# The first three MLP blocks of a decoder trunk: another order of TensorE's products

## The chip, the core and the metric

The kernel runs on one core of a Trainium2 chip. A core has five engines that run side by side and wait for each other through semaphores: TensorE (PE in the profile) multiplies matrices, VectorE (DVE) and ScalarE (ACT) work on single elements, GpSimd (POOL) and SyncE (SP) here mainly issue DMA transfers. TensorE reads from SBUF and writes to PSUM, which has 8 banks; a matmul can add to what stands in a bank. The metric is the time of one execution in microseconds of the device.

## The reference

Two decoder layers over 512 tokens of width 1024, in float32. The change lies in the MLP, which each layer ends with:

```python
def sq_relu_mlp(xn, w_up, w_down):
    hid = jnp.square(jax.nn.relu(xn @ w_up))
    return hid @ w_down

for i in range(DEPTH):                      # DEPTH = 2
    ...                                     # a mixer: attention in layer 0, gated linear attention in layer 1
    x = x + sq_relu_mlp(rms_norm(x, norm_mlp[i]), mlp_w_up[i], mlp_w_down[i])
```

`w_up` is 1024 x 4096 and `w_down` 4096 x 1024.

## The kernel before

**Numbers.** TensorE's fast format holds fewer bits than float32, so each operand is cut into a high and a low part: ScalarE rounds to the high part (`wh`, line 112), VectorE subtracts it and keeps the low part (`wl`, line 115). A product of two such operands is three matmuls: high with high, high with low, low with high. The function `piece` cuts one piece of weights; there are three buffers each for `wh` and `wl`.

**Blocks.** `up_block(b)` computes 512 of the 4096 hidden features for all tokens, for b = 0 to 7. It treats the product as a 2 x 2 block product and does it with seven products instead of eight, in the manner of Strassen and Winograd. The weights of a block are four quarters a11, a12, a21, a22 of 512 rows by 256 columns (512 KB each), and sums of them; the inputs are quarters of the normed x and sums of those, ready before the MLP starts (`x0h` to `x7l`, and `T0h` to `T3l` for the sums T1 to T4). One product, `product(bank, weights, name, begin)`, is 24 matmuls of 128 x 128 weights by 256 columns: 16 with `wh`, then 8 with `wl`. The steps of a block, each with its product:

- s1: product 11 of a11, into a bank x1 (three such banks, tag "u"). Its result also seeds the running sum: `seed` has ScalarE copy it into the bank b2. There is one such bank (tag "seed").
- s2: product 21 of a12, added to x1. `finish` then scales it and clips it on VectorE (line 889) and squares it on ScalarE (line 890), into the hidden tile q.
- s5: product T1 of s = a21 + a22, into a bank x5; ScalarE copies it away as p5. In blocks 2 to 7 this step also loads a12, computes s (line 931) and has GpSimd's queue load a11 on top of a21.
- s6: VectorE makes s := s + a11 (line 948). Product T2 of s is added to the running sum b2; ScalarE copies the sum away as u2.
- s3: VectorE makes a12 := a12 + s (line 954). Product 22 of a12 is added to x5; VectorE adds u2 to it (line 957), and `finish`.
- s7: product T3 of a21 (a11 was added to it on loading) is added to the running sum b2; VectorE reads b2 and adds p5 (line 963), and `finish`.
- s4: product T4 of a22 is added to the running sum b2, and `finish`.

An engine that reads a bank and TensorE that writes it wait for each other.

**Order.** The order in which the steps are called sets the order of instructions on each engine. Blocks 0 and 1 begin interleaved (s1, s1, s2, s2); block 1's first sum is kept as p1 in SBUF, since the bank b2 belongs to block 0 then, and `seed` copies it in at its s6. From there each block ran to its end: s5, s6, s3, s7, s4. From block 2 on, steps of `down_block` (the second matrix, products of hidden tiles `h` with 48 matmuls each) stand between the steps. Weights of block 2 and later come through five buffers (tag "raw", 512 KB each); SP's queue issues the loads in order, each when a buffer is free.

Of the kernel before, what the change touches and what calls it, by code (L numbers as in the profile page):

```python
# [15 lines left out]
ALU = mybir.AluOpType  # L16
# [33 lines left out]
def trunk_kernel(ctx: ExitStack, tc: tile.TileContext, t_in: dict, out: bass.AP, out_row: bass.AP):  # L50
    nc = tc.nc
    PE, ACT, DVE, POOL, SP = nc.tensor, nc.scalar, nc.vector, nc.gpsimd, nc.sync
# [15 lines left out]
    def pool_of(name):  # L68
        return now[name][1]
# [3 lines left out]
    def uname(s):  # L73
        count[0] += 1
        return f"{s}_{count[0]}"
# [34 lines left out]
    def split(src, hi, lo, hi_eng=ACT, lo_eng=DVE, order=lambda i: i):  # L110
        if hi_eng is ACT:
            raised.append(order(ACT.activation(hi, src, AF.Copy)))  # L112
        else:
            hi_eng.tensor_copy(hi, src)
        return lo_eng.tensor_tensor(lo, src, f(hi), ALU.subtract)  # L115
# [29 lines left out]
    def piece(raw, a, n, order=lambda i: i):  # L145
        hi = sb.tile([P, a, n], F32R, tag="wh", bufs=3, name=uname("wh"))
        lo = sb.tile([P, a, n], F32R, tag="wl", bufs=3, name=uname("wl"))
        cut_at.append(split(raw, hi, lo, order=order))
        return hi, lo
# [658 lines left out]
    def mlp(layer, nrm, nxt, final=False):  # L808
        w_up, w_dn = t_in["mlp_w_up"][layer], t_in["mlp_w_down"][layer]
        quad = nrm.quad  # L810
        NB = FF // FB
# [11 lines left out]
        def matmuls(p, w, k0, ks, ms, x, begin, end):  # L823
            def one(i, j, k, m, start, stop):
                return PE.matmul(  # L825
                    p[:, m * TH : (m + 1) * TH],
                    w[i][:, k - k0, m * P : (m + 1) * P],
                    x[k][j],
                    start=start,
                    stop=stop,  # L830
                    skip_group_check=True,
                )

            steps = [(k, m) for k in ks for m in ms]
            for k, m in steps:
                i = one(0, 0, k, m, begin and k == 0 and m % 2 == 0, False)
                if (k, m) == steps[0]:
                    tc.keep_in_program_order(i)
                one(0, 1, k, m, False, False)
            for k, m in steps:  # L840
                one(1, 0, k, m, False, end and k == 3)
# [3 lines left out]
        def up_block(b):  # L845
            fh, s = b % 2, b // 2
            q = []

            def outputs():
                q.extend(pool_of("down").tile([P, 4, TH], F32, tag="q", bufs=6, name=uname("q")) for _ in range(2))  # L850
                Q[s, fh] = q

            def unit(half, trail):
                if half and b < 2:
                    return wide[b][trail]
                return fill(up.tile([P, KH, 256], F32, tag="raw", bufs=5, name=uname("raw")), half, trail)

            def rows(half, trail):
                c0 = b * FB + half * 256
                return w_up[trail * 512 : trail * 512 + 512, c0 : c0 + 256].rearrange("(k p) n -> p k n", p=P)  # L860

            def fill(t, half, trail):
                with tc.issue_after(wide["last"].ins) if "last" in wide and b > 1 else nullcontext():
                    i = SP.dma_start(t, rows(half, trail))
                if half and b < 2:
                    wide["last"] = i
                return t

            def fill_sums(s):
                v["s"] = s  # L870
                fill(s, 1, 0)
                joint(s, 1, 1)
                fill(wide[b][0], 1, 0)
                joint(wide[b][0], 0, 0)
                fill(wide[b][1], 1, 1)

            def joint(t, half, trail):
                POOL.dma_start(t, rows(half, trail), accum_op=ALU.add)  # L878

            fills.append(fill_sums)  # L880

            def product(p, a, name, begin):
                w = v.pop(name) if name in v else piece(a, KH, 256)
                matmuls(p, w, 0, range(KH), range(2), quad[name], begin, True)

            def finish(c, half, tk):
                qs = q[tk is second][:, 2 * half : 2 * half + 2]
                r = nrm.rstd[:, tk].unsqueeze(1).to_broadcast([P, 2, TH])
                DVE.scalar_tensor_tensor(qs, c, 0.0, r, ALU.min if half else ALU.max, ALU.mult)  # L889
                ACT.activation(qs, qs, AF.Square)  # L890

            def pairs(t):
                return t.rearrange("p (j t) -> p j t", j=2)

            def mt():
                return pool_of("down").tile([P, 512], F32, tag="mt", bufs=4, name=uname("mt"))

            v = made[b] = {}

            def s0():  # L900
                v["a11"], v["a12"] = unit(0, 0), unit(0, 1)
                if b == 0:
                    for name, a in (("11", v["a11"]), ("21", v["a12"])):
                        v[name] = piece(a, KH, 256)
                else:
                    w = v["11"] = tuple(up.tile([P, KH, 256], F32R, tag=f"T{KH - 1}{x}", name=uname("w")) for x in "hl")
                    split(v["a11"], *w)

            def s1():
                outputs()  # L910
                if "a11" not in v:
                    v["a11"] = unit(0, 0)
                a = v["a11"]
                v["a21"], v["a22"] = unit(1, 0), unit(1, 1)
                v["x1"] = bank("u")
                product(v["x1"], a, "11", True)
                if b == 1:
                    v["p1"] = mt()
                    ACT.activation(v["p1"], v["x1"], AF.Copy)
                else:  # L920
                    seed(v["x1"])

            def seed(src):
                v["b2"] = pool_of("mps").tile([P, 512], F32, tag="seed", name=uname("ps"))
                ACT.activation(v["b2"], src, AF.Copy)

            def s5():
                if "s" not in v:
                    v["s"] = up.tile([P, KH, 256], F32, tag="raw", bufs=5, name=uname("raw"))
                    v["a12"] = unit(0, 1)  # L930
                    DVE.tensor_tensor(v["s"], v["a21"], v["a22"], ALU.add)  # L931
                    joint(v["a21"], 0, 0)
                s = v["s"]
                v["x5"] = bank("u")
                product(v["x5"], s, "T1", True)
                v["p5"] = mt()
                ACT.activation(v["p5"], v["x5"], AF.Copy)

            def s2():
                if "a12" not in v:  # L940
                    v["a12"] = unit(0, 1)
                product(v["x1"], v["a12"], "21", False)
                finish(pairs(v["x1"]), 0, first)

            def s6():
                if b == 1:
                    seed(v["p1"])
                DVE.tensor_tensor(v["s"], v["s"], v["a11"], ALU.add)  # L948
                product(v["b2"], v["s"], "T2", False)
                v["u2"] = mt()  # L950
                ACT.activation(v["u2"], v["b2"], AF.Copy)

            def s3():
                DVE.tensor_tensor(v["a12"], v["a12"], v["s"], ALU.add)
                product(v["x5"], v["a12"], "22", False)
                c = q[1][:, 0:2]
                DVE.tensor_tensor(c, pairs(v["x5"]), pairs(v["u2"]), ALU.add)
                finish(c, 0, second)

            def s7():  # L960
                product(v["b2"], v["a21"], "T3", False)
                c = q[1][:, 2:4]
                DVE.tensor_tensor(c, pairs(v["b2"]), pairs(v["p5"]), ALU.add)  # L963
                finish(c, 1, second)

            def s4():
                product(v["b2"], v["a22"], "T4", False)
                finish(pairs(v["b2"]), 1, first)

            return [s0, s1, s2, s5, s6, s3, s7, s4] if b < 2 else [s1, s5, s2, s6, s3, s7, s4]  # L970

        def down_block(s):
            last = s == NB // 2 - 2
# [155 lines left out]

        made = {}  # L1130
        blocks = [up_block(b) for b in range(NB)]
        for b in range(2):
            blocks[b].pop(0)()
# [29 lines left out]
        for b in range(2):  # L1163
            blocks[b].pop(0)()
        downs = []
        for b in range(NB):
            for i, step in enumerate(blocks[b]):
                step()
                if downs and (i % 2 or (b % 2 and i == 6)):
                    downs.pop(0)()  # L1170
            if b % 2 and b < NB - 1:
                downs += down_block(b // 2)
# [579 lines left out]
```

## Time and profile before

| | |
|---|---|
| three runs | 1067.56, 1068.91 and 1069.22 us, median 1068.91 |
| profiled execution | 1068.29 us; its span, from the first to the last instruction, 1066.6 us |
| TensorE busy | 1048.6 us, 7322 matmuls |
| VectorE busy | 856.7 us |
| ScalarE busy | 640.1 us |
| products at line 825, up and down, of both layers | about 192 to 465 us and 739 to 1012 us of the span |
| TensorE's granted clock, mean | 0.996 of full speed |

A row of the timeline gives the start in us, the duration, the engine, the line, the operation, the tiles written and read, the count, and in brackets the idle time before it with what ended it. Matmuls overlap in their pipeline: a row's duration of 0.28 us is not its cost, which is the distance from start to start.

### The profile page before, as it was taken

The numbers are of one execution on the slowest core, as the hardware profiler recorded it, in microseconds if no ns is written. First come the engines' busy times: TensorE is split into PE (matmuls) and PEld (weight loads), VectorE is DVE, ScalarE is ACT, GpSimd is POOL, SyncE is SP. The second block draws the span as 40 slices with busy tenths as digits, with TensorE's granted clock in tenths as the row PEclk, the third lists the DMA queues.
The fourth block names the chain that finished last, engine by engine and source line by source line (L and its number), as shares of the span: only waits on it lengthen the run. The fifth ranks groups of instructions, "written<-read, shape, count | busy, mean of one in ns | idle before, by whom it ended". The sixth has DMA issues, their size and how long they took to land.

```text
span 1066.6 us, 17924 instructions
## 1 busy us (share of the span) xinstructions
PE 1048.6 (98%) x7322; PEld 967.8 (91%) x7322; DVE 856.7 (80%) x1185; ACT 640.1 (60%) x934; POOL 77.9 (7%) x104
## 2 busy tenths in 40 slices
PE   8999999999999999999999999999999999999997
PEld 6788888989999999998788888888999999999986
DVE  6789879899899789966565654668999799799865
ACT  6577645665666776654334734655666667775734
POOL 6400000000000000030000000001000000000000
PEclk9999999999999999999999999999999999999999
DMA  6412016865554663351122212238564555653412
GB/s 204 105 50 79 1 40 196 180 179 137 166 139 132 178 147 117 94 193 43 50 80 80 80 48 71 80 98 216 163 137 139 169 129 158 187 128 103 139 39 80
DMA packets 113874, 126.76 MB, mean 119 GB/s; under 512 B 8592, under 2 KB 85664, under 8 KB 113792
## 3 DMA queue, kind: packets, MB, share of 16 engines
q1 hardware_dynamic: 98048, 107.62, 31.7%
q0 software_dynamic: 13792, 16.80, 10.1%
q10 hardware_dynamic: 1952, 1.21, 0.4%
q8 instruction: 57, 0.93, 0.4%
q14 instruction: 25, 0.20, 0.1%
HBM read 123.51 MB, written 2.10 MB: 118 GB/s over the span
## 4 chain that ended last, share of the span: by engine, by line
PE 93%; DVE 5%; DMA 1%; issue 1%; ACT 0%; SPq 0%; DVEq 0%
PE ps L825 46%; PE ps L120 13%; PE ps L122 13%; PE ps L121 13%; PE ps L137 2%; DVE wl L115 2%; PE ps L1406 2%; DMA wraw_ckv<-in_mla_w_in_dram 1%; PE ps L1445 0%; PE ps L684 0%; DVE raw L948 0%; PE ps L685 0%; PE ps L683 0%; PE ps L682 0%; PE ps L681 0%
## 5 line engine op out<-in xcount | busy, mean ns | idle before, releaser
L112 ACT ACTIVATE wh<-raw 128x1024 fp32r<-128x1024 f32 x208 | 219.7, 1059 | 139.6 <-PE ps L825 86.1
L115 DVE TENSOR_TENSOR wl<-raw,wh 128x1024 fp32r<-128x1024 f32 x208 | 251.5, 1220 | 22.6 <-ACT wh L112 22.0
L825 PE MATMUL ps<-h,wh 128*128 128x256 f32 x1344 | 166.6, 276 | 0.0
L825 PEld LDWEIGHTS ps<-h,wh 128*128 128x128 f32 x1344 | 159.2, 188 | 0.0
L120 PE MATMUL ps<-set,wh 128*128 128x512 f32 x232 | 91.6, 395 | 1.7 <-ACT set L245 1.7
L121 PE MATMUL ps<-set,wh 128*128 128x512 f32 x232 | 91.5, 394 | 1.0 <-DVE set L246 0.9
L825 PE MATMUL ps<-h,wl 128*128 128x256 f32 x672 | 90.4, 277 | 1.8 <-DVE wl L115 1.8
L122 PE MATMUL ps<-set,wl 128*128 128x512 f32 x232 | 91.3, 394 | 0.0
L112 ACT ACTIVATE wh<-wraw 128x1024 fp32r<-128x1024 f32 x41 | 43.0, 1057 | 73.7 <-PE ps L122 41.5
L825 PEld LDWEIGHTS ps<-h,wl 128*128 128x128 f32 x672 | 82.7, 188 | 2.2 <-DVE wl L115 2.2
L878 POOL DMA_DIRECT2D raw<-in_mlp_w_up_dram x20 | 25.8, 1290 | 701.2 <-DVE raw L931 309.0
L890 ACT ACTIVATE q<-q 128x512 f32<-128x512 f32 x64 | 40.3, 630 | 52.9 <-DVE q L889 52.6
L115 DVE TENSOR_TENSOR h<-q,h 128x1024 fp32r<-128x1024 f32 x44 | 53.7, 1222 | 8.3 <-ACT h L112 8.3
L120 PE MATMUL ps<-wh,set 128*128 128x512 f32 x144 | 59.6, 414 | 0.0
L115 DVE TENSOR_TENSOR wl<-wraw,wh 128x1024 fp32r<-128x1024 f32 x41 | 50.3, 1229 | 10.6 <-ACT wh L112 10.5
L122 PE MATMUL ps<-wh,set 128*128 128x512 f32 x144 | 56.3, 391 | 0.0
L121 PE MATMUL ps<-wl,set 128*128 128x512 f32 x144 | 56.2, 390 | 0.0
L121 PEld LDWEIGHTS ps<-set,wh 128*128 128x128 f32 x232 | 44.1, 190 | 11.0 <-DVE set L246 1.9
L120 PEld LDWEIGHTS ps<-set,wh 128*128 128x128 f32 x232 | 43.8, 189 | 10.9 <-ACT set L245 1.9
L122 PEld LDWEIGHTS ps<-set,wl 128*128 128x128 f32 x232 | 44.0, 190 | 9.1
L112 ACT ACTIVATE h<-q 128x1024 fp32r<-128x1024 f32 x44 | 46.0, 1049 | 0.8 <-DVE q L1024 0.8
L825 PE MATMUL ps<-T0h,wh 128*128 128x256 f32 x128 | 32.7, 280 | 5.0 <-DVE q L963 5.0
(512 smaller groups left out, 2779.0 us busy)
## 6 DMA issues: line engine op xcount, KB each, us to landing
raw<-in_mlp_w_down_dram SPq DMA_DIRECT2D x38, 1024.0 KB, 5.2
raw<-in_mlp_w_up_dram SPq DMA_DIRECT2D x68, 512.0 KB, 5.7
wraw<-in_gla_w_in_dram SPq DMA_DIRECT2D x11, 1024.0 KB, 5.2
raw<-in_mlp_w_up_dram POOLq DMA_DIRECT2D x20, 512.0 KB, 6.4
raw<-in_mlp_w_down_dram POOLq DMA_DIRECT2D x6, 1024.0 KB, 9.0
wraw<-in_mla_w_o_dram SPq DMA_DIRECT2D x8, 512.0 KB, 4.9
wraw<-in_gla_w_o_dram SPq DMA_DIRECT2D x8, 512.0 KB, 4.7
xT<-in_x_dram SPq DMA_DIRECT2D x6, 256.0 KB, 7.9
```

The lines of the kernel that those rows point to most:

```text
L112: raised.append(order(ACT.activation(hi, src, AF.Copy)))
L115: return lo_eng.tensor_tensor(lo, src, f(hi), ALU.subtract)
L120: PE.matmul(psum, wh, xh, start=start, stop=False, **kw)
L121: PE.matmul(psum, wh, xl, start=False, stop=False, **kw)
L122: PE.matmul(psum, wl, xh, start=False, stop=stop, **kw)
L137: PE.transpose(psum, src, ident[: src.shape[0], : src.shape[0]])
L825: return PE.matmul(p[:, m * TH : (m + 1) * TH], w[i][:, k - k0, m * P : (m + 1) * P], x[k][j], start=start, stop=stop, skip_group_check=True,)
L878: POOL.dma_start(t, rows(half, trail), accum_op=ALU.add)
L890: ACT.activation(qs, qs, AF.Square)
L1406: PE.matmul(p[:, t * 64 : (t + 1) * 64].rearrange("p (n c) -> p n c", c=m), k[:, sl], later, start=True, stop=True)
```

## The change

Three things move, in the first three blocks of each layer. The order of steps of blocks 0 and 1 is interleaved: after s7 of block 0 comes s5 of block 1, then s4 of block 0. In block 1 step s3 (product 22) goes ahead of s6 (T2); the sum s + a11 is then made in s3, and the rest of s3 that needs u2 (`third`) at the end of s6. Block 2 keeps its first sum as p1 like block 1; its s1 goes ahead of s7 of block 1, and its s2 ahead of s4 of block 1 and of its own s5. The three down steps beside block 2 come after its s5, s6 and s7. Step s5 itself is unchanged: in block 2 it still finds no sum `s`, and so loads a12 again, which s2 has loaded by then.

```diff
-                if b == 1:
+                if b in (1, 2):
                     v["p1"] = mt()
                     ACT.activation(v["p1"], v["x1"], AF.Copy)
...
+            def twice():
+                DVE.tensor_tensor(v["s"], v["s"], v["a11"], ALU.add)
+
             def s6():
-                if b == 1:
+                if b in (1, 2):
                     seed(v["p1"])
-                DVE.tensor_tensor(v["s"], v["s"], v["a11"], ALU.add)
+                if b != 1:
+                    twice()
                 product(v["b2"], v["s"], "T2", False)
                 v["u2"] = mt()
                 ACT.activation(v["u2"], v["b2"], AF.Copy)
+                if b == 1:
+                    third()
 
             def s3():
+                if b == 1:
+                    twice()
                 DVE.tensor_tensor(v["a12"], v["a12"], v["s"], ALU.add)
                 product(v["x5"], v["a12"], "22", False)
+                if b != 1:
+                    third()
+
+            def third():
                 c = q[1][:, 0:2]
                 DVE.tensor_tensor(c, pairs(v["x5"]), pairs(v["u2"]), ALU.add)
                 finish(c, 0, second)
...
-            return [s0, s1, s2, s5, s6, s3, s7, s4] if b < 2 else [s1, s5, s2, s6, s3, s7, s4]
+            if b == 1:
+                return [s0, s1, s2, s5, s3, s6, s7, s4]
+            return [s0, s1, s2, s5, s6, s3, s7, s4] if b == 0 else [s1, s2, s5, s6, s3, s7, s4] if b == 2 else [s1, s5, s2, s6, s3, s7, s4]
...
-        for b in range(NB):
-            for i, step in enumerate(blocks[b]):
+        for b in (0, 0, 0, 0, 1, 0, 1, 1, 2, 1, 2, 1):
+            blocks[b].pop(0)()
+        assert not blocks[0] and not blocks[1]
+        downs = down_block(0)
+        for b in range(2, NB):
+            for i, step in enumerate(blocks[b], 7 - len(blocks[b])):
                 step()
-                if downs and (i % 2 or (b % 2 and i == 6)):
+                if downs and (i in (2, 3, 5) if b == 2 else i % 2 or (b % 2 and i == 6)):
                     downs.pop(0)()
```

The products of blocks 0 to 2 in TensorE's order, with the block's number behind the name (dn: a down step of two 24-matmul halves):

```text
before  T1.0 T2.0 22.0 T3.0 T4.0 T1.1 T2.1 22.1 T3.1 T4.1 11.2 T1.2 dn 21.2 T2.2 dn 22.2 T3.2 dn T4.2
after   T1.0 T2.0 22.0 T3.0 T1.1 T4.0 22.1 T2.1 11.2 T3.1 21.2 T4.1 T1.2 dn T2.2 dn 22.2 T3.2 dn T4.2
```

TensorE in layer 0, at the end of T3 of block 0; `ps_2289` is the bank of the running sum, `wh_2525` holds the weights of T4. Before:

```order
L825 MATMUL ps_2289<-T2h_2129,wl_2495 128x256 x2
L825 MATMUL ps_2289<-T3h_2332,wl_2495 128x256 x2
L825 MATMUL ps_2289<-T0h_1953,wh_2525 128x256
L825 MATMUL ps_2289<-T0l_1954,wh_2525 128x256
L825 MATMUL ps_2289<-T1h_2041,wh_2525 128x256
```

The same place now; `ps_2525` is the bank x5 of block 1 and `wh_2526` its weights for T1:

```order
L825 MATMUL ps_2289<-T2h_2129,wl_2495 128x256 x2
L825 MATMUL ps_2289<-T3h_2332,wl_2495 128x256 x2
L825 MATMUL ps_2525<-T0h_1953,wh_2526 128x256
L825 MATMUL ps_2525<-T0l_1954,wh_2526 128x256
L825 MATMUL ps_2525<-T1h_2041,wh_2526 128x256
```

T1 of block 1 has moved between T3 and T4 of block 0.

VectorE at the same place, from the split for T3 of block 0 on (`wl_2495`): `raw_2251` is the sum s, of block 0 first and then of block 1, `raw_2157` and `raw_2159` are a11 and a12 of block 1, `q_2263` and `q_2262` are hidden tiles. Before:

```order
L115 TENSOR_TENSOR wl_2495<-raw_2249,wh_2494 128x1024
L115 TENSOR_TENSOR wl_2526<-raw_2249,wh_2525 128x1024
L957 TENSOR_TENSOR q_2263<-ps_2400,mt_2460 128x512
L115 TENSOR_TENSOR wl_2557<-raw_2251,wh_2556 128x1024
L889 SCALAR_TENSOR_TENSOR q_2263<-q_2263,rstd_2337 128x512
L948 TENSOR_TENSOR raw_2251<-raw_2251,raw_2157 128x1024
L963 TENSOR_TENSOR q_2263<-ps_2289,mt_2429 128x512
L954 TENSOR_TENSOR raw_2159<-raw_2159,raw_2251 128x1024
L889 SCALAR_TENSOR_TENSOR q_2263<-q_2263,rstd_2337 128x512
L115 TENSOR_TENSOR wl_2590<-raw_2251,wh_2589 128x1024
L889 SCALAR_TENSOR_TENSOR q_2262<-ps_2289,rstd_2337 128x512
```

Now, where lines 946, 962, 969 and 975 are what lines 948, 954, 957 and 963 were:

```order
L115 TENSOR_TENSOR wl_2495<-raw_2249,wh_2494 128x1024
L115 TENSOR_TENSOR wl_2527<-raw_2251,wh_2526 128x1024
L946 TENSOR_TENSOR raw_2251<-raw_2251,raw_2157 128x1024
L962 TENSOR_TENSOR raw_2159<-raw_2159,raw_2251 128x1024
L969 TENSOR_TENSOR q_2263<-ps_2400,mt_2460 128x512
L115 TENSOR_TENSOR wl_2557<-raw_2249,wh_2556 128x1024
L889 SCALAR_TENSOR_TENSOR q_2263<-q_2263,rstd_2337 128x512
L975 TENSOR_TENSOR q_2263<-ps_2289,mt_2429 128x512
L115 TENSOR_TENSOR wl_2589<-raw_2159,wh_2588 128x1024
L889 SCALAR_TENSOR_TENSOR q_2263<-q_2263,rstd_2337 128x512
L115 TENSOR_TENSOR wl_2619<-raw_2251,wh_2618 128x1024
L889 SCALAR_TENSOR_TENSOR q_2262<-ps_2289,rstd_2337 128x512
```

Both sums of block 1 (the rows that write `raw_2251` and `raw_2159`) have moved ahead of the read of 22 and of the read of the running sum after T3 (the rows that read `ps_2400` and `ps_2289`).

SP's queue from the first load for block 2 on; the rows of the up weights are a11, a21, a22 and a12 of block 2. Before:

```order
L864 DMA raw_2714<-in_mlp_w_up_dram 128x4x256
L864 DMA raw_2716<-in_mlp_w_up_dram 128x4x256
L864 DMA raw_2718<-in_mlp_w_up_dram 128x4x256
L981 DMA raw_2787<-in_mlp_w_down_dram 128x4x512
L864 DMA raw_2752<-in_mlp_w_up_dram 128x4x256
L981 DMA raw_2911<-in_mlp_w_down_dram 128x4x512
L981 DMA raw_2913<-in_mlp_w_down_dram 128x4x512
```

Now:

```order
L864 DMA raw_2653<-in_mlp_w_up_dram 128x4x256
L864 DMA raw_2655<-in_mlp_w_up_dram 128x4x256
L864 DMA raw_2657<-in_mlp_w_up_dram 128x4x256
L864 DMA raw_2721<-in_mlp_w_up_dram 128x4x256
L995 DMA raw_2819<-in_mlp_w_down_dram 128x4x512
L864 DMA raw_2784<-in_mlp_w_up_dram 128x4x256
L995 DMA raw_2915<-in_mlp_w_down_dram 128x4x512
L995 DMA raw_2917<-in_mlp_w_down_dram 128x4x512
```

The load of a12 for s2 (`raw_2721`) stands ahead of the first down weights, and a second load of a12 (`raw_2784`) where the only one stood. SP's whole list has 148 rows instead of 146.

## The prediction

> **What bounds the kernel now.** I read the page first, then who TensorE waits for, the chain of waits, a table by stretches, and the timeline of TensorE. The page's busy shares and its chain:
> ```profile
> span 1066.6 us, 17924 instructions
> PE 1048.6 (98%) x7322; PEld 967.8 (91%) x7322; DVE 856.7 (80%) x1185; ACT 640.1 (60%) x934; POOL 77.9 (7%) x104
> PE 93%; DVE 5%; DMA 1%; issue 1%; ACT 0%; SPq 0%; DVEq 0%
> ```
> TensorE (PE) is busy 98% of the span, so only two things can shorten the time: an idle gap of TensorE that closes, or a faster pace of its matmuls. Who ends its gaps, longest total first (line waited for: us in total, times, longest):
> ```profile
> PE ps L825 <- DVE q L963: 5.0, 4, 1.5
> PE ps L825 <- DVE wl L115: 1.8, 2, 1.0
> PE ps L120 <- ACT set L245: 1.7, 1, 1.7
> ```
> The first row is the one the change aims at: four waits, two in each layer's MLP, for VectorE's (DVE's) read of the running sum after T3 (line 963). Their places, the start of each product of blocks 0 and 1 in layer 0 (start, duration, engine; a product is 24 matmuls and only its first is shown), and from layer 1 the two waits, two starts before the first of them and two after it:
> ```profile
> 203.87 0.28 PE L825 MATMUL ps<-T0h,wh 128*128 128x256 f32 x1
> 206.69 0.28 PE L825 MATMUL ps<-T0h,wh 128*128 128x256 f32 x1
> 209.52 0.28 PE L825 MATMUL ps<-x4h,wh 128*128 128x256 f32 x1
> 212.35 0.28 PE L825 MATMUL ps<-T0h,wh 128*128 128x256 f32 x1
> 216.84 0.39 PE L825 MATMUL ps<-T0h,wh 128*128 128x256 f32 x1 [1.50 <-DVE q L963]
> 219.69 0.28 PE L825 MATMUL ps<-T0h,wh 128*128 128x256 f32 x1
> 222.41 0.28 PE L825 MATMUL ps<-T0h,wh 128*128 128x256 f32 x1
> 225.13 0.28 PE L825 MATMUL ps<-x4h,wh 128*128 128x256 f32 x1
> 227.85 0.28 PE L825 MATMUL ps<-T0h,wh 128*128 128x256 f32 x1
> 231.73 0.39 PE L825 MATMUL ps<-T0h,wh 128*128 128x256 f32 x1 [1.00 <-DVE q L963]
> 234.57 0.28 PE L825 MATMUL ps<-x0h,wh 128*128 128x256 f32 x1
> 751.20 0.28 PE L825 MATMUL ps<-T0h,wh 128*128 128x256 f32 x1
> 754.03 0.28 PE L825 MATMUL ps<-T0h,wh 128*128 128x256 f32 x1
> 764.17 0.39 PE L825 MATMUL ps<-T0h,wh 128*128 128x256 f32 x1 [1.50 <-DVE q L963]
> 767.02 0.28 PE L825 MATMUL ps<-T0h,wh 128*128 128x256 f32 x1
> 769.74 0.28 PE L825 MATMUL ps<-T0h,wh 128*128 128x256 f32 x1
> 779.05 0.39 PE L825 MATMUL ps<-T0h,wh 128*128 128x256 f32 x1 [0.99 <-DVE q L963]
> ```
> These rows show a second thing, which the change touches without meaning to: **TensorE has two paces**. Before the first wait a product takes 2.82 to 2.83 us (206.69 - 203.87, 209.52 - 206.69, 212.35 - 209.52; 118 ns a matmul); after it 2.72 us (222.41 - 219.69 and the next two; 113 ns). Layer 1 does the same: 754.03 - 751.20 = 2.83 before its first wait, 769.74 - 767.02 = 2.72 after it. T products and 22 show both paces, so it is no property of the product. The slow pace is there before these rows begin, and the first wait ends it in both layers. TensorE's granted clock (the number after the five engines) is 1.00 on both sides, so the clock is not it:
> ```profile
> 203.80:215.00 11.20, 11.20 (x97) 11.20 (x97) 9.85 (x11) 7.13 (x9) 0.00 (x0) 1.00 0.53 149
> 217.00:230.00 13.00, 13.00 (x116) 13.00 (x116) 12.73 (x13) 9.14 (x13) 1.27 (x1) 1.00 0.74 183
> ```
> The third busy figure is VectorE's: 12.73 of 13.00 us. It is nearly full, so the closing of a TensorE gap can run into VectorE.
>
> Why VectorE is late at the first wait (its rows, then ScalarE's copy that seeds the running sum of block 1, SP's issue of two down weights, and the DMA issues of up weights: count, size, us to landing):
> ```profile
> 212.62 0.69 DVE L957 TENSOR_TENSOR q<-ps,mt 128x512 f32<-128x512 f32 x1 [1.08 <-PE ps L825]
> 213.23 1.22 DVE L115 TENSOR_TENSOR wl<-raw,wh 128x1024 fp32r<-128x1024 f32 x1
> 214.36 0.69 DVE L889 SCALAR_TENSOR_TENSOR q<-q,rstd 128x512 f32<-128x512 f32 x1
> 214.96 1.22 DVE L948 TENSOR_TENSOR raw<-raw,raw 128x1024 f32<-128x1024 f32 x1
> 216.10 0.68 DVE L963 TENSOR_TENSOR q<-ps,mt 128x512 f32<-128x512 f32 x1
> 216.70 1.22 DVE L954 TENSOR_TENSOR raw<-raw,raw 128x1024 f32<-128x1024 f32 x1
> 221.15 0.58 ACT L925 ACTIVATE ps<-mt 128x512 f32<-128x512 f32 x1
> 219.68 8.23 SPq L981 DMA_DIRECT2D raw<-in_mlp_w_down_dram  x2
> raw<-in_mlp_w_up_dram SPq DMA_DIRECT2D x68, 512.0 KB, 5.7
> ```
> T3 of block 0 ends about 215.2. The read of line 963 stands behind a sum of weights (line 948), starts at 216.10 and lasts 0.68; T4 adds to the same bank and may start only then, 216.84. From start to start VectorE spends 1.13 us on a 1024-wide instruction and 0.60 on a 512-wide one; I use these below.
>
> **The change part by part.** The sum is made against the profiled execution, 1068.29 us; the median of the runs is 0.62 higher.
>
> 1. *The four waits.* The gap to the next product less a product: block 0, 216.84 - 212.35 - 2.83 = 1.66, and T4 itself takes 219.69 - 216.84 = 2.85 instead of 2.72, 0.13 for refilling; block 1, 231.73 - 227.85 - 2.72 = 1.16 and 234.57 - 231.73 - 2.72 = 0.12. Together 3.07 us a layer, 6.1 in both. This goes if VectorE's read is done while the product put between runs.
>
> 2. *Is it done?* I lay VectorE's new order (in the section on the change) end to end. Through the split for T1 of block 1 it is the old order, done at about 211.5. Then two sums of weights, each on the result before it, to 213.8; the read of 22 of block 0 to 214.4; the split for T4 to 215.6; the scaling to 216.2; the read of T3 ends 216.9. TensorE, at the slow pace, runs T1 of block 1 from 215.2 to 218.0 and only then needs that bank for T4: 1.1 us to spare. Next splits for 22 and T2 of block 1 end 217.9 and 219.7, before 220.8 and 223.7. T4 of block 0 ends 220.8; VectorE reads it by 221.7, ScalarE squares it and seeds the bank with a copy like that at 221.15, which ends 222.9; T2 of block 1 needs it at 223.7: 0.7 to spare. The same count puts the read after T3 of block 1 at 233.1 to 233.8, with T4 at 235.0; at the fast pace of TensorE 0.6 is left. So I see no new wait, but no margin over 1.2 us either.
>
> 3. *Block 2.* Its product 11 now comes before T3 of block 1, and 21 before T4. 21 needs a12 early: its buffer is block 1's a11, free after the sum that ends at 212.7; with 5.7 us to landing it is there at 218.4, and ScalarE splits it at about 225.7. Step s5 of block 2 then loads a12 a second time, since the sum `s` does not exist yet: one DMA of 512 KB more per layer. On SP's queue it stands ahead of two loads of down weights; its buffer is block 1's a12, free after the split for 22 at 217.9, so it goes at about 218, lands by 223.8 and is wanted at about 243. The load behind it is issued at 219.8, as late as before (before, the next one went at 219.68). The DMA engines are half busy (0.53, 0.74 above). I cost it at nothing; its cover is some 19 us of TensorE work. The earlier copies on ScalarE cost nothing either: it has 9.14 busy of 13 us.
>
> 4. *The slow pace.* Without the first wait, nothing resets it there. The products from T1 of block 1 to T1 of block 2, nine of them (T1, T4 of block 0, 22, T2, 11, T3, 21, T4, T1), run at 2.83 instead of 2.72: 9 x 0.11 = 0.97 us a layer, 1.9 in both. Between the bounds of 0 (reset at once) and the whole rest of the MLP (below) I take the first product of the down block as its end. Its rows and the product after it:
> ```profile
> 240.01 0.75 PE L825 MATMUL ps<-h,wh 128*128 128x256 f32 x5
> 245.62 0.28 PE L825 MATMUL ps<-x4h,wh 128*128 128x256 f32 x1
> 248.35 0.28 PE L825 MATMUL ps<-T0h,wh 128*128 128x256 f32 x1
> 327.23 0.40 PE L825 MATMUL ps<-h,wh 128*128 128x256 f32 x2
> 439.11 1.98 PE L825 MATMUL ps<-h,wh 128*128 128x256 f32 x16
> 442.06 0.62 PE L825 MATMUL ps<-h,wl 128*128 128x256 f32 x3 [0.97 <-DVE wl L115]
> ```
> That down product takes 5.61 us for 48 matmuls, 117 ns each, and the one after it 2.73 us: TensorE came out of a stretch of slow matmuls without any wait. I expect it to do so from the slow pace too.
>
> The sum: 1068.29 - 6.1 + 1.9 = 1064.1 us. Carried to the median of the runs it is 1064.7. I say 1064.5.
>
> [...]
>
> **The rivals.**
>
> *No slow pace to pay* (17%): the pace resets at T1 of block 1 or at block 2's product 11, whose operands have not been seen in that state. Then 1068.29 - 6.1 = 1062.2. For it: at a wait the state ends within one product (T4 of block 0 took 2.85 with its refilling, the next 2.72), so little is needed to end it. Against: it went unbroken through the three changes of product from 203.87 to 212.35.
>
> *The slow pace outlives the down product* (15%), and the kernel gets slower. The next first product of a down block comes at 327.23, 87 us later; to it are 87 / 2.72 = 32 products, 3.5 us a layer: 1064.1 + 7.0 = 1071.1. To the wait at 442 above, 200 us or 73 products, 8.0 us a layer: 1080.1. It decides from 2.1 / 0.11 = 19 products past the down product on. For it: nothing but a wait has been seen to end this pace itself. Against: the recovery at 245.62.
>
> *The gain is eaten* (14%): VectorE's margins of 0.6 to 1.2 us are overrun, by one late transfer or copy, or VectorE, whose end of the layer is the wait at 442.06, does not move up with TensorE. Each wait that comes back costs 1 to 1.7 us; all of them back give 1068.3, half of them 1066.
>
> **How the numbers follow.** My forecast has 54%, the rivals 17, 15 and 14. The range takes in the forecast, no slow pace, and the gain eaten in part or whole: 1061.8 to 1069.0; only the slower rival is left out. About 0.2%, 2.1 us, is what a measurement of this kernel can tell from no change. Faster: the forecast, no slow pace and a quarter of the eaten gain, 0.74. Same: the rest of the eaten gain, 0.11. Slower: 0.15.
>
> **What the profile of the changed kernel would show.** Item 1: no row of TensorE waiting for the read after T3 (line 975 now), and T4 of block 0 starting near 218.0. Item 2: if wrong, a wait of TensorE at 218.0, 223.7 or 235.0 that names lines 975, 889 or the seeding copy. Item 3: if wrong, ScalarE or VectorE waiting for a DMA of up or down weights before 250. Item 4: products 2.83 us apart from 203.9 to about 240.6, where the first down product should start (it starts at 240.01 now with one product fewer, 2.73 us, before it: 2.1 us gained), and 2.72 apart after it. Products still 2.83 apart at 260 would mean the slower rival; 2.72 apart from 218 on, the first one.

## The result, and the profile after

The changed kernel takes 1069.86 us (median of 21 runs, 1068.78 to 1071.83), the kernel before on the same chip 1068.48 (21 runs, 1067.34 to 1070.45). The ratio is 1.0015, with a 95% interval of 1.0008 to 1.0021: slower by 1.4 us where 4.4 us less were forecast, and 0.9 us above the top of the range. The profiled execution has a span of 1067.3 us.

The page, answering the lines shown of before, first the span, then the busy times of the engines, then the chain that ended last:
```profile
span 1067.3 us, 17937 instructions
PE 1055.7 (99%) x7322; PEld 975.6 (91%) x7322; DVE 857.3 (80%) x1185; ACT 642.3 (60%) x936; POOL 76.3 (7%) x104
PE 7%; DVE 0%; ACT 0%; issue 0%; DVEq 0%
```
TensorE has the same 7322 matmuls and is busy for 7.1 us more (1055.7 against 1048.6). The chain was followed through 7% of this span only, so I use its starts and waits instead. Of the rows on who ends TensorE's gaps, these two answer rows shown of before (line waited for: us in total, times, longest):
```profile
PE ps L120 <- ACT set L245: 1.5, 1, 1.5
PE ps L825 <- DVE wl L115: 1.2, 2, 0.6
```
The row of four waits for VectorE's read after T3 (5.0 us) is gone, and no new one stands in its place. The idle time was closed and came back as busy time: the same matmuls are slower. Starts of TensorE's products in layer 0 (a product is 24 matmuls, the down product from 240.20 has 48):
```profile
203.45 0.28 PE L825 MATMUL ps<-T0h,wh 128*128 128x256 f32 x1
206.28 0.28 PE L825 MATMUL ps<-T0h,wh 128*128 128x256 f32 x1
...
214.76 0.28 PE L825 MATMUL ps<-T0h,wh 128*128 128x256 f32 x1
217.58 0.28 PE L825 MATMUL ps<-T0h,wh 128*128 128x256 f32 x1
220.41 0.28 PE L825 MATMUL ps<-x4h,wh 128*128 128x256 f32 x1
223.24 0.28 PE L825 MATMUL ps<-T0h,wh 128*128 128x256 f32 x1
...
234.54 0.28 PE L825 MATMUL ps<-T0h,wh 128*128 128x256 f32 x1
237.37 0.28 PE L825 MATMUL ps<-T0h,wh 128*128 128x256 f32 x1
...
240.20 2.03 PE L825 MATMUL ps<-h,wh 128*128 128x256 f32 x16
...
245.80 0.28 PE L825 MATMUL ps<-T0h,wh 128*128 128x256 f32 x1
...
248.62 0.40 PE L825 MATMUL ps<-h,wh 128*128 128x256 f32 x2
...
327.77 0.40 PE L825 MATMUL ps<-h,wh 128*128 128x256 f32 x2
...
333.38 0.28 PE L825 MATMUL ps<-x4h,wh 128*128 128x256 f32 x1
...
336.11 0.28 PE L825 MATMUL ps<-T0h,wh 128*128 128x256 f32 x1
```
Products stand 2.83 us apart up to the first down product at 240.20, as forecast, and still 2.82 apart behind it (248.62 - 245.80), which was the mark of the slower rival. Only behind the next first product of a down block, 327.77 to 333.38, is a product back at 2.73 (336.11 - 333.38). TensorE between these two down products, in layer 0 and in layer 1, of the kernel before (start:end, length, busy time and number of matmuls, granted clock, share of the DMA engines, GB/s):
```profile
246.00:327.00 81.00, 81.00 (x717) 1.00 0.55 150
795.00:876.00 81.00, 81.00 (x717) 1.00 0.53 147
```
and of the changed kernel:
```profile
246.00:327.00 81.00, 81.00 (x690) 1.00 0.61 161
795.00:876.00 81.00, 81.00 (x690) 1.00 0.60 160
```
In the same 81 us, never idle and at clock 1.00, TensorE does 27 matmuls fewer: 81 / 717 is 113 ns each, 81 / 690 is 117. That is where the gain went.

The stretch as a whole: from the full-precision matmul of line 255 to the first matmul behind the MLP (line 120), layer 0, before and then after:
```profile
197.36 0.59 PE L255 MATMUL ps<-acc,inv 128*128 128x512 f32 x1
464.85 0.39 PE L120 MATMUL ps<-hh,wh 128*128 128x512 f32 x1
```
```profile
196.94 0.59 PE L255 MATMUL ps<-acc,inv 128*128 128x512 f32 x1
465.00 0.39 PE L120 MATMUL ps<-hh,wh 128*128 128x512 f32 x1
```
267.49 us before and 268.06 after, +0.57. Taken the same way, layer 1 gives +0.75. Together 1.3 us, as much as the medians differ by (1.4). The spans of the two profiled executions differ by 0.7 us only: the rest of the program took 0.6 us less in the second.

### The profile page after: what moved, and what is told of

Read it like the earlier page. It is cut to its first block, busy times and chain, and to the rows that moved or that the text cites. A ratio compares the mean times of both kernels' runs of the same rounds, so it can differ in the third digit from the quotient of the medians.

```text
span 1067.3 us, 17937 instructions
## 1 busy us (share of the span) xinstructions
PE 1055.7 (99%) x7322; PEld 975.6 (91%) x7322; DVE 857.3 (80%) x1185; ACT 642.3 (60%) x936; POOL 76.3 (7%) x104
## 5 line engine op out<-in xcount | busy, mean ns | idle before, releaser
L121 PE MATMUL ps<-hl,wh 128*128 128x512 f32 x96 | 37.4, 389 | 0.0
```

Source lines behind the costliest of these rows:

```text
L121: PE.matmul(psum, wh, xl, start=False, stop=False, **kw)
```

## The experiments

Each run was timed beside the kernel before on its own chip; that one's median was 1069.21 us for the first four, 1069.98 for the next four and 1068.05 for the last four, with executions of up to 1072.9, 1077.1 and 1070.2 us, so neither the times nor the ratios compare closely across these groups. Where runs are compared below, it is by their traces: the two stretches from line 255 to line 120, taken as above, make 534.8 us together in the kernel before and 536.1 in the changed one. The theory at the start, P: TensorE keeps its pace until something ends it, and a wait ends the slow one.

**1. The first wait back.** Two steps exchanged, so that T4 of block 0 follows T3 of block 0 again:
```
-        for b in (0, 0, 0, 0, 1, 0, 1, 1, 2, 1, 2, 1):
+        for b in (0, 0, 0, 0, 0, 1, 1, 1, 2, 1, 2, 1):
```


> The changed kernel with one pair of steps exchanged back: T4 of block 0 follows T3 of block 0 directly, so the first wait of each layer is back (1.66 us), the second stays away. Theory P (TensorE keeps its pace until something ends it, and a wait ends the slow one): TensorE goes from 118 to 113 ns a matmul at that wait, about 217, and stays there; against the changed kernel that costs 1.7 us a layer and saves 0.108 us on each of some 37 products (8 to the down product at 240, 29 from 246 to 328), 4.0 us a layer: 1069.9 + 3.4 - 8.0 = 1065.3, below the kernel before by the second wait, some 2.5 us. Rival Q (the new order itself, its operands or the load of VectorE keeps the matmuls slow, history does not matter): the pace stays 118 behind the wait and the time is 1069.9 + 3.4 = 1073.

Measured: 1068.83 us, ratio 0.9993 (0.9979 to 1.0008), between the two. The order made a further wait which nobody had asked for, of 22 of block 1 for ScalarE's copy. The first matmuls behind the waits, in layers 0 and 1, and then TensorE behind the first wait of layer 0, behind its second, and behind the second of layer 1:
```profile
216.38 0.39 PE L825 MATMUL ps<-T0h,wh 128*128 128x256 f32 x1 [1.50 <-DVE q L975]
223.17 0.38 PE L825 MATMUL ps<-x4h,wh 128*128 128x256 f32 x1 [1.06 <-ACT mt L937]
764.12 0.38 PE L825 MATMUL ps<-T0h,wh 128*128 128x256 f32 x1 [1.50 <-DVE q L975]
770.91 0.39 PE L825 MATMUL ps<-x4h,wh 128*128 128x256 f32 x1 [1.06 <-ACT mt L937]
```
```profile
217.00:221.50 4.50, 4.50 (x43) 1.00 0.44 123
224.00:242.00 18.00, 18.00 (x155) 1.00 0.57 161
772.00:788.00 16.00, 16.00 (x143) 1.00 0.52 139
```
(Counts take in two or three matmuls that overlap an end of the window.) The first wait does end the slow pace, 118 to 113 ns. But the second, at the same product and with the same 1.06 us in both layers, leaves TensorE at 118 ns in layer 0 (18 us / 153) and at 113 in layer 1 (16 us / 141). In layer 0 it turned a fast TensorE slow. So a wait does not end the slow pace as such; P falls in that form. What stood from here on is theory D: a break in the even stream draws the pace anew, and it is then kept to the next break (I say draws because the runs do not show what decides which of the two it becomes). Q falls too, since the pace changed at 217 within the same order of work.

**2. Product 11's weights shifted by 64 bytes.** This product of block 1 runs at 120 ns a matmul in both kernels, alone of all, and the slow pace is seen behind it. By the addresses that the program gives its tiles, nearly all products of the MLP have their weights at 32 and their moving operand at 96 modulo 128 bytes; this one has both at 96.
```
-                    w = v["11"] = tuple(up.tile([P, KH, 256], F32R, tag=f"T{KH - 1}{x}", name=uname("w")) for x in "hl")
+                    w = v["11"] = tuple(
+                        up.tile([P, KH * 256 + 32], F32R, tag=f"T{KH - 1}{x}", name=uname("w"))[:, 16 : 16 + KH * 256].rearrange("p (k n) -> p k n", k=KH)
+                        for x in "hl"
+                    )
```
These weights lie in the tiles of T3. The tiles get 128 bytes longer, and by the addresses T3's low part now stands 128 bytes further on than before, modulo 256.

> The changed kernel with the two weight buffers of block 1's product 11 shifted by 64 bytes, and nothing else. In both kernels that product is the only one at 120 ns a matmul and the slow pace is first seen behind it. Theory R (it starts the slow pace): with the shift product 11 runs at 113, no slow pace is seen before the down product at about 240, and with the four waits gone as well: some 45 products at 0.108 us less, 4.9 us a layer, about 1060. Rival F (the few full-precision matmuls that stand a little behind it, line 255, start the slow pace): product 11 alone gets faster, 24 x 7 ns a layer, and the time is that of the changed kernel less 0.3, 1069.5. Rival Q (order, operands or VectorE's load make it slow): 1069.5 too. Where VectorE cannot follow the faster TensorE, waits of up to 1 us a product would show instead and eat part of it.

Measured: 1063.16 us, ratio 0.9942 (0.9923 to 0.9961). TensorE in product 11, behind the matmuls of line 255, and behind the first down product:
```profile
194.00:196.40 2.40, 2.40 (x23) 1.00 1.17 239
198.50:238.50 40.00, 40.00 (x342) 1.00 0.61 161
246.00:256.00 10.00, 10.00 (x91) 1.00 0.91 228
```
Product 11 is now fast, and the slow pace starts all the same, behind the matmuls of line 255: theory R had the wrong cause and F the right one. Yet the time is near R's, because the first down product, which TensorE now reached at 239.78 in place of 240.20, this time left it fast. Whether that product ends the slow pace is no property of the product alone. In layer 1 the pace turned fast already at 754, inside a T product, with no listed wait and no odd offset there. The edit did more than its purpose, though: with T3's low part moved, T products take 113.9 ns a matmul in the fast pace in place of 113.3. So which part of the edit brought the faster pace is not shown.

**3. No odd offset.** The first down product of each superblock reads its moving operand at 64 modulo 128 bytes, the others at 96. Here all read it at 96:
```
-                    c = 0 if turn[1] != s else 40
+                    c = 40
```


> The changed kernel with the first down product of each superblock reading its moving operand at the offset that all others have (40 columns) instead of 0. In the changed kernel the slow pace ended with such a product at 328 and 876. Theory P (the pace lasts until something ends it; these products, unlike the others in where their operand stands, are such a thing): nothing ends it now before the wait near 441 of each layer, so some 40 more products at 0.108 us, 4.3 us a layer, less the 1 us of that wait: about 1069.9 + 7 = 1077. Rival S (it ended by itself or by the change of work around 328): the slow stretch ends at 328 as before, 1069.5 to 1069.9.

Measured: 1079.18 us, ratio 1.0086 (1.0066 to 1.0105), P's and D's figure (8.3 us over the changed kernel by the stretches, 7 expected). TensorE between the first two down blocks and behind the second:
```profile
266.00:326.00 60.00, 60.00 (x511) 1.00 0.58 151
336.00:386.00 50.00, 50.00 (x427) 1.00 0.50 146
```
Slow to the end of the MLP, in both layers. Taking the odd operand away takes the end of the slow pace away: S falls.

**4. The same shift as in 2, in the kernel before.**

> The kernel before with the same shift by 64 bytes of the weight buffers of block 1's product 11. Theory R: no slow pace from 194 to the first wait at 217, so some 8 products at 0.108 us less and 0.16 us on product 11, 1.0 us a layer, as far as VectorE is early by as much at the wait: 1066.5 to 1067.5 against 1068.5. Rivals F and Q: 0.2 us a layer or nothing, 1068.1 to 1068.5.

Measured: 1069.79 us, ratio 1.0002 (0.9989 to 1.0014): nothing, as F and Q said. The four waits stand there unchanged, at 5.0 us, so what 2 gained came from the slow stretch and not from product 11. In layer 1 the slow pace ended at 756, before the first wait and again inside a T product.

**5. One more odd offset.** The first and the third down product of each superblock read at 64:
```
-                    c = 0 if turn[1] != s else 40
+                    turn[2] = turn[2] + 1 if turn[1] == s else 0
+                    c = 0 if turn[2] < 2 else 40
```


> The changed kernel with a second down product of each superblock, the third one, reading its operand at the odd offset as the first does. Theory D (the pace is drawn anew wherever the even stream of matmuls is broken, by a wait or by such a product, and is kept from there to the next break; the first down product drew the slow pace again here): the third one, some 10 us behind the first, draws again and more often fast than slow (five of the six such products seen so far left TensorE fast); if fast, some 28 products of layer 0 and of layer 1 gain 0.108 us, and the time is 1069.9 - 6.0 = 1064, and half of that if one layer alone. Rival L (the slow stretch lasts until 328 whatever stands in it, by the work of that stretch): 1069.9 or 0.1 more.

Measured: 1066.53 us, ratio 0.9956 (0.9938 to 0.9974). By the stretches it is 3.1 us under the changed kernel, half of the 6.0 expected. Before the third down product at 260, and behind it:
```profile
247.00:258.00 11.00, 11.00 (x96) 1.00 0.94 254
266.00:326.00 60.00, 60.00 (x532) 1.00 0.60 159
```
The pace turns from 118 to 113 ns at that product, in both layers. L falls: in the same work, at the same time, and with the DMA engines as busy (0.60), one operand's place decides it. The gain is smaller because 22 products stand there and not 28, because the two odd products of a layer that now stand in the fast pace cost 0.17 us each, and because the wait at the end of the MLP grew from the 1.2 us of the changed kernel:
```profile
PE ps L825 <- DVE wl L115: 2.1, 2, 1.7
```

**6 to 8. The moving operands at 32.** x4 to x7 and T0 to T3 of the up products stand at 32 modulo 128 bytes, in the changed kernel (6) and in the kernel before (7); in 8 the down operands are moved as well.
```
-            hi, lo = (pool.tile([P, n], F32R, tag=f"x{j}{x}", name=uname(f"x{j}{x}")) for x in "hl")
+            hi, lo = (
+                pool.tile([P, n + 16 * (f"{j}{x}" in (f"{KH}h", f"{2 * KH - 1}l"))], F32R, tag=f"x{j}{x}", name=uname(f"x{j}{x}"))[:, 16 * (f"{j}{x}" == f"{KH}h") :][:, :n]
+                for x in "hl"
+            )
```
and in 8 as well
```
-                    h = dp.tile([P, 8 * TH + 40], F32R, tag="h1", name=uname("h"))
-                    c = 0 if turn[1] != s else 40
+                    h = dp.tile([P, 8 * TH + 56], F32R, tag="h1", name=uname("h"))
+                    c = 56
...
-                    h = dp.tile([P, 2, 4, TH], F32R, tag="h0", name=uname("h"))
+                    h = dp.tile([P, 8 * TH + 16], F32R, tag="h0", name=uname("h"))[:, : 8 * TH].rearrange("p (i k t) -> p i k t", i=2, k=4)
```
The first tile gets longer, so that all that stand behind it in memory move. By the addresses x1 to x3 and the weights of block 1's product 11 thereby stand at 32 too, and x0 stays at 96.

> The changed kernel with the moving operands of all up products (x4 to x7, T0 to T3) 64 bytes further on, nothing else. In both kernels nearly all products of the MLP have their weights at 32 and their moving operand at 96 modulo 128 bytes, and only such products have shown two paces. Theory A (the two paces belong to that pair of places): with the moving operand at 32 the up products have one pace, 113 ns a matmul or less, and no slow stretch stands from 197 to 240 nor, since the first down product is then not entered from the slow pace, behind it: some 46 products of each layer gain 0.108 us, 1069.9 - 9.9 = 1060, as far as VectorE, 98% busy there, can follow; waits of TensorE for it of up to 1 us each would then be seen. Rival N (place does not matter, the slow pace follows whatever breaks the stream): slow behind the matmuls of line 255 as before, 1063 to 1070.

> The kernel before with the same 64 bytes. Beside the changed kernel with them it prices the change where no pace can differ. Theory A: the up products run at one pace, some 8 products of each layer gain 0.108 us as far as the reads after T3 allow, the four waits stay at some 5 us: 1067 to 1068.5; and the changed kernel stands lower than this one by the waits with their refill, 6.1 us less what VectorE cannot follow, 4 to 6 us. Rival N: 1068.5, with the changed kernel within 2 us of it.

> The changed kernel with the moving operands of the up products and of all down products at 32 modulo 128 bytes, so that none of them stands at 96 or at the odd offset. Theory A: one pace from 197 to the end of the MLP in both layers, the eight first down products of superblocks fast as well (48 x 3.5 ns each): 1059, a little under the kernel in which only the up products are moved; if the pace of that place is under 113 ns, lower. Rival N: slow from 197 on with nothing to end it, 1077 as in the run without the odd offset.

Measured: 6, 1075.44 us, ratio 1.0049 (1.0029 to 1.0069); 7, 1081.68 us, ratio 1.0097 (1.0065 to 1.0129); 8, 1086.46 us, ratio 1.0139 (1.0109 to 1.0168). From 203.5 to 227.5 in 6, and the 60 us of mixed up and down products in 8:
```profile
203.50:227.50 24.00, 24.00 (x204) 1.00 0.60 181
```
```profile
266.00:326.00 60.00, 60.00 (x505) 1.00 0.57 150
```
The products at 32 have one pace, as theory A said, but the slow one: 118 to 119 ns in 6's up products, 118 to 120 in all of 8. I had taken it for the fast one without ground. The down products of 6, at 96 or 64, took 113 to 118 ns. N is wrong as well.

6 and 7 together are the price of the change where both kernels have nearly the same pace. 7 has the four waits, 6 has none:
```profile
PE ps L828 <- DVE q L966: 4.5, 4, 1.5
```
The stretch of layer 0, first in 6 and then in 7 (rows as above):
```profile
199.00 0.59 PE L255 MATMUL ps<-acc,inv 128*128 128x512 f32 x1
469.73 0.39 PE L120 MATMUL ps<-hh,wh 128*128 128x512 f32 x1
```
```profile
196.62 0.59 PE L255 MATMUL ps<-acc,inv 128*128 128x512 f32 x1
470.36 0.39 PE L120 MATMUL ps<-hh,wh 128*128 128x512 f32 x1
```
270.73 against 273.74: 3.01 us a layer, 6.0 in both (layer 1, taken the same way, gives 3.0). The medians differ by 6.2. The waits with their refill are 2.8 us a layer of it; the other 0.2 is one down product (at 251 and at 805 in 7) that is slow in 7 and fast in 6.

**9 and 12. x4 at the odd offset.** x4 alone stands at 64, as the first down products' operands do; it heads products 21 and 22, and one of these comes right behind line 255.
```
-            hi, lo = (pool.tile([P, n], F32R, tag=f"x{j}{x}", name=uname(f"x{j}{x}")) for x in "hl")
+            hi, lo = (
+                pool.tile([P, n + 32 * (j == KH)], F32R, tag=f"x{j}{x}", name=uname(f"x{j}{x}"))[:, 24 * (j == KH) :][:, :n]
+                for x in "hl"
+            )
```


> The changed kernel with the moving operand x4 alone at the odd offset (64 modulo 128 bytes), where the first down products have theirs. x4 stands at the head of products 21 and 22, from the first one behind the matmuls of line 255 on. Theory D (such an operand lets the pace be drawn anew, mostly fast, and it is then kept): fast from about 201 on in place of 328, some 44 products of each layer at 0.108 us less, up to 1069.9 - 9.5 = 1060.4, less what VectorE cannot follow (waits of TensorE, each of which may draw the slow pace again); if one layer alone draws fast, 1065. Rival K (only the down product's own work lets it go): slow to 240 and to 328 as in the changed kernel, 1069.9.

> The kernel before with x4 alone at the odd offset. Theory D: fast from about 201 to the first wait at 217, where TensorE then waits longer unless VectorE is early by as much: 1067 to 1068.5; and each wait draws the pace anew, by a chance of about one in five for the slow one, which would cost 0.9 us to the down product at 240 and up to 4 more behind it. Rival K: 1068.5, the same trace as before.

Measured: 9, the changed kernel with it, 1063.22 us, ratio 0.9950 (0.9937 to 0.9962); 12, the kernel before with it, 1070.65 us, ratio 1.0020 (1.0011 to 1.0029). Two starts and a longer stretch of 9, and then what followed the first wait of 12 in layer 0 and in layer 1:
```profile
203.65 0.28 PE L828 MATMUL ps<-T0h,wh 128*128 128x256 f32 x1
206.37 0.28 PE L828 MATMUL ps<-T0h,wh 128*128 128x256 f32 x1
```
```profile
266.00:326.00 60.00, 60.00 (x529) 1.00 0.60 158
```
```profile
217.50:225.00 7.50, 7.50 (x66) 1.00 0.64 202
766.00:772.00 6.00, 6.00 (x55) 1.00 0.69 230
```
In 9 T products are 2.72 us apart from 203.65 on, 36 us before the first down product: K falls. By the stretches it is 6.0 us under the changed kernel where 9.5 were expected, because each of the 32 products with x4 now takes 2.82 in place of 2.72, 3.2 us in all, which the expectation left out. VectorE kept up: no wait of TensorE stands in these blocks. In 12 the first wait of layer 0 drew the slow pace (7.5 us / 64 is 117 ns), that of layer 1 the fast one: the mild case of the bad draw that the expectation named. That is not the main reason why 12 is slower than the kernel before: by the stretches it is so by 0.7 us in layer 0 and by 0.4 in layer 1, where the draw was fast, and its products with x4 take 2.82 us as well.

**10. No second load of a12.**
```
-                    v["a12"] = unit(0, 1)
+                    if "a12" not in v:
+                        v["a12"] = unit(0, 1)
```


> The changed kernel without the second load of a12 in block 2 (its sum is then made from the first). Item 3 of the prediction: the load costs nothing, no TensorE start moves, 1069.9 as the changed kernel. Rival (its 512 KB per layer delay a load that is waited for, or disturb the matmuls): 1 us or more less.

Measured: 1071.02 us, ratio 1.0024 (1.0015 to 1.0033), no gain; the two stretches make 536.1 us as in the changed kernel, and the slow pace stands there as well:
```profile
266.00:326.00 60.00, 60.00 (x512) 1.00 0.60 158
```

**11. Three edits together**: 2, 5 and 9 in one.

> The changed kernel with product 11's weights shifted, x4 at the odd offset and a second odd down product in each superblock, to give the fast pace a chance at 201, 240 and 260. Theory D: fast from 201 in both layers, 1059 to 1061; if the draw at 201 fails, fast from 240 or 260 on: 1063 to 1064. Rival K: 1063 to 1064 as well, with the slow pace to 240 in the trace.

Measured: 1065.41 us, ratio 0.9966 (0.9953 to 0.9978). It is fast from 205 on in layer 0 and from 759 on in layer 1, and yet behind 2 and 9, by 0.5 and 0.8 us by the stretches. A likely reason, not tested by itself: the odd operands cost 0.1 us a product, and there are more of them.

Of the versions that beat both kernels (2, 5, 9 and 11), 2 and 9 are the fastest, at 0.994 to 0.995 of the kernel before.

## Why the prediction was wrong, step by step

**Item 1, the four waits (6.1 us): right.** They are gone, and with the pace held nearly equal, in 6 and 7, they are worth 5.7 us.

**Item 2, VectorE is in time: right, with the margins worked out.** VectorE's reads after T3 of blocks 0 and 1, and ScalarE's seeding copy:
```profile
215.89 0.68 DVE L975 TENSOR_TENSOR q<-ps,mt 128x512 f32<-128x512 f32 x1
232.63 0.68 DVE L975 TENSOR_TENSOR q<-ps,mt 128x512 f32<-128x512 f32 x1
221.87 0.59 ACT L925 ACTIVATE ps<-mt 128x512 f32<-128x512 f32 x1
```
The first read ends at 216.57 and T4 starts at 217.58: 1.0 us to spare, 1.1 forecast. The copy ends at 222.46, T2 of block 1 starts at 223.24: 0.8, 0.7 forecast. The second read ends at 233.31 and T4 starts at 234.54: 1.2, as forecast for the slow pace.

**Item 3, block 2's loads cost nothing: right.** No wait names them, and without the second load the time is no better.

**Item 4, the slow pace: half right.** Up to the first down product the forecast held: nine products at 2.83, then the down product at 240.20. From line 255 that is 43.26 us (240.20 - 196.94) against 42.65 before (240.01 - 197.36), but with one product of 2.83 more ahead of it: 2.2 us gained, where 2.1 were forecast. The step that failed is the next one: "I take the first product of the down block as its end", and the ground for it, "TensorE came out of a stretch of slow matmuls without any wait. I expect it to do so from the slow pace too." The kernel before has six such products, and all were entered from the fast pace. Here, entered from the slow pace, it left TensorE slow, so 29 more products (245.80 to 327.77) took 0.108 us more, 3.1 us a layer, of which the wait at the end of the layer's MLP gave back 0.3: its row went from 1.8 to 1.2 us for both layers. -2.2 + 3.1 - 0.3 is +0.6 a layer, where the stretches gave +0.57 and +0.75.

How far that ground carried can be counted in the traces of both kernels and of the runs other than 6, 7, 8 and 12. The down products at 64 that were entered from the fast pace all left it fast, 52 of 52. Of the 14 entered from the slow pace 8 left TensorE fast and 6 slow. Those six are the ones at 240 and 788 in the changed kernel and in runs 5 and 10, which have the same work up to there. What follows the product does not decide it: in run 1 the same T2 follows, and the pace is fast. So the step was a guess that fails in some places and holds in others, and why it fails in these stays open.

**The rivals.** What came is the second, with its first sub-case: the pace lasts to the next first product of a down block, which that rival put at 327.23, 32 products and 1071.1 us. It had 15%. (Its 32 products take in the down product itself, which lasts 5.6 us in both kernels; 29 had to be paid.) Its "nothing but a wait has been seen to end this pace itself" was the better reading of the same rows; its sub-case of 442 is what run 3 made. The ground against the first rival ("a wait ends it within one product, so little is needed") was as weak as that for the forecast: a wait does not end it surely.

Both kernels depended on this draw. The kernel before was fast behind 217 because its waits, all four, happened to draw the fast pace. The change took away idle time and with it those draws.

## What to carry to other kernels

Before a gap of TensorE is closed, look at the pace of its matmuls on both sides of the gap: if they differ, the gap does something besides costing time. A state seen to end in some way after one entry may not be assumed to end so after another; give its duration the bounds of the next events that could end it, and let the range take in the worst. When idle time falls and busy time rises by as much, count the matmuls in equal windows before looking for a new wait.

## What the runs showed of the hardware

Matmuls of one shape (128 x 128 by 256 columns, split operands) take 113 or 118 ns at a granted clock of 1.00 with no wait between them, and the pace in force is kept over hundreds of them (696 in a row in the changed kernel, some 2300, the rest of a layer's MLP, in run 3). It goes with where the operands stand. With weights at 32 and the moving operand at 96 modulo 128 bytes both paces occur; with the moving operand at 32 the products showed 118 to 120 ns alone (runs 6 to 8); with all of it at 64 (the first down products), 117 on average; with both at 96, 120.

The pace mostly changes at a break of the even stream. The pair of full-precision matmuls of line 255 was followed by the slow one in both layers of every kernel that kept the moving operands behind it at 96. A wait of the same length can give either (1.06 us in run 1, fast in one layer and slow in the other). A down product at 64 kept the fast pace each time and ended the slow one in 8 of 14 cases, as counted above. In layer 1 of runs 2 and 4 the pace changed inside a T product, with T3's low part moved by 128 bytes as the only oddity known there. In the changed kernel, by the starts of its matmuls, the down product at 240.20 fell into steps of 117, 117 and 116 ns and left TensorE slow; those that left it fast showed steps of four values, such as 118, 120, 113 and 116. Which step of TensorE's weight loading and reading this is, and why those places matter, these runs do not show. Nor was a wait tried by itself, with the order of the work unchanged. Each version was traced in one execution, so that a draw comes out the same in the next one is not shown either; that the changed kernel, 5 and 10 agree at 240 and at 788 speaks for it.

The Trainium skill's "SBUF — State Buffer", section "Operand start alignment", gives a rule for where an operand may start and says that it is about legality and not speed. The runs here show a speed too: with operands moved by 64 bytes the two stretches of the changed kernel took 5.4 us more in 6, and with product 11's weights moved by 64 and T3's low part by 128 they took 5.7 us less in 2.
